# Moving the start addresses of a streaming encoder's matmul operands relative to the weights, by padding

## The chip, the cores and the metric

The kernel runs on one core of one Trainium2 chip. The metric is the time of one execution on the device, in microseconds. Where a profile is quoted, it is of one execution of the same program, with its own time.

## The reference, cut to what matters

The reference is one layer of a streaming encoder for 256 prompt tokens and 32 sample tokens, 288 together, at a model width of 2048, in float32. Nearly all of its arithmetic is products of the 288 tokens with weight matrices:

```python
h = rmsnorm(x, norm_in)
(a_q, a_k, a_v, i_q, i_k, i_w, a_z, b_z, b_xbc, b_dt, m_q, m_z, gates) = split_cols(h @ w_in)
...
mkv = rmsnorm(mem_prompt, norm_mem) @ w_mem_kv          # 256 memory tokens
...
merged = g_a * (ya @ w_pa) + g_b * (yb @ w_pb) + g_m * (ym @ w_pm)
return x + merged @ w_o, ...
y = rmsnorm(..., norm_final)
```

Between them stand three branches: sparse attention over keys picked by an indexer (`ya`), a Mamba-2 scan (`yb`) and cross-attention into the memory tokens (`ym`). They are small beside the products and run on the other engines and in short matmuls between those of the products.

## The kernel before, in words

Activations lie transposed: 128 channels on the partitions, and for each block k of 128 channels a row of 288 tokens along the partition, 1,152 bytes. A tile of 16 blocks is [128, 16, 288]. Weights come from memory as strips: 128 output columns by 1,024 input channels, 512 KB at a time, into `wr`.

Precision is kept by splitting. Each float32 number is written as a high part (`fp32r`, a rounded form) and a low part, the rest. `split_hi` (L119) and `split_lo` (L122) do this for activations. `convert` (L175 to L201) does it for weights: it takes the next job, issues the load of `wr` (L185), lets ScalarE write the high weights `wh` (L199) and VectorE the low ones `wl` (L200). So every product is three: high activations by high weights, low activations by high weights, high activations by low weights.

`strip` (L132 to L150) makes the jobs of a product. In a job of 1,024 channels there are 24 matmuls into one PSUM tile `ps`: for each of eight blocks i a pair, the high rows and then the low rows against `wh`, and after these the eight high rows against `wl` in the reverse order. The stationary operand (the one loaded by LDWEIGHTS) is the 128x128 block of weights, the moving operand is the row of 288 tokens; every matmul has its own weight load. The blocks go in the order `EVEN_ODD = (0, 2, 4, 6, 1, 3, 5, 7)`, and the weights of odd blocks lie in a second half of their tile:

```python
wh = wpool.tile([P, 1088], F32R, tag="wh", name="wh")                        # L186
wh = bass.AP(tensor=wh.tensor, offset=wh.offset, ap=[wh.ap[0], [544, 2], [P, 4], [1, P]])   # L191
```

The second half begins 544 elements, 2,176 bytes, behind the first. A row of 288 tokens is 1,152 bytes. Modulo 256 both of them put the odd ones 128 bytes behind the even ones.

`run` (L258) works the list of jobs off: for each, it converts the weights of a later one, issues the 24 matmuls, and calls `step`, which lets the side work (attention, scan, norms: Python generators) issue its next piece. The order of jobs is: memory keys (`w_mk`, strips over the memory tokens, rows of 256 tokens, 1,024 bytes), memory values (`mv_block`, L152: here blocks of `memh` and `meml` are the loaded operand, and 512 columns of weights move), then `w_in` in 133 strips of two jobs, with `w_pm`, `w_pa`, `w_pb` and `w_o` (16 strips each) where their inputs are ready.

The moving tiles are these. `xh` and `xl`, high and low rows of the normed input, come from the pool `const` (L76, L77), which is laid out in the order of the calls, one tile behind the other; `mgh` and `mgl`, the merged branches, take the same places at the end (L1063, L1064). The others are slots A to H of the pool `big`, given out by `slot` (L64): A and B hold `memraw` and `memh` at first and the pair `yb` for `w_pb` later; C holds `meml` and later other things; E and F hold the memory keys and values, then the pair `ym` for `w_pm`, then the pair `ya` for `w_pa`; D, G and H hold float32 tiles that no high or low row is in. Between `const` and `big` lies `wpool` with three buffers each of `wr` (4,096 bytes), `wh` and `wl` (4,352 bytes, 17 times 256); pools lie in the order of L41 to L46. In this layout `xh`, `xl`, every `wh` and `wl`, and each slot start at 128 modulo 256.

Of the kernel before, what the change touches and what calls it, by code (L numbers as in the profile page):

```python
# [7 lines left out]
F32 = mybir.dt.float32  # L8
F32R = mybir.dt.float32r
# [4 lines left out]
P = 128  # L14
TP = 256
TS = 32
T = TP + TS
# [16 lines left out]
def step_kernel(ctx, tc, ins, outs):  # L34
    nc = tc.nc
    V, S, G, PE = nc.vector, nc.scalar, nc.gpsimd, nc.tensor
    PS = bass.MemoryType.PSUM

    const = ctx.enter_context(tc.tile_pool(name="const", bufs=1))
    wpool = ctx.enter_context(tc.tile_pool(name="wpool", bufs=3))  # L40
    big = ctx.enter_context(tc.tile_pool(name="big", bufs=1))  # L41
# [19 lines left out]
    def st(n=8):  # L61
        return stp.tile([P, n], F32, tag="st", name="st")

    def slot(tag, shape, dt=F32):  # L64
        return big.tile(shape, dt, tag=tag, name=tag)

    def mm(out, lhsT, rhs, start=True, stop=True):
        PE.matmul(out, lhsT, rhs, start=start, stop=stop)  # L68
# [1 line left out]

    N = Names()
    N.memraw = slot("A", [P, 16, 256])
    N.memh = slot("B", [P, 16, 256], F32R)
    N.meml = slot("C", [P, 16, 256], F32R)
    N.x = slot("D", [P, 16, T])
    xh = const.tile([P, 16, T], F32R, name="xh", tag="xh")  # L76
    xl = const.tile([P, 16, T], F32R, name="xl", tag="xl")  # L77
    X = (xh, xl)

    S.preload_act_table_set("natural_log_exp_and_others")  # L80
    nc.sync.dma_start(N.memraw[:, 0:4], ins["memT"][:, 0:4])
    cols = const.tile([P, 288], F32, name="cols")
    S.dma_start(cols[:, 0:272], ins["cols"])
    g_mem, g_in, g_ssm, g_fin, d_col = (cols[:, 16 * i:16 * i + 16] for i in range(5))
    cw = cols[:, 80:176].rearrange("p (c i) -> p c i", c=24)
# [439 lines left out]
    dt = const.tile([P, 96], F32, name="dt")  # L525
# [534 lines left out]
    proj(N_G, ev_gb)  # L1060

    def begin_pb():
        N.mg = (const.tile([P, 16, T], F32R, name="mgh", tag="xh"),  # L1063
                const.tile([P, 16, T], F32R, name="mgl", tag="xl"))  # L1064

    def ev_pb(j):
# [9 lines left out]
        return f  # L1076

    hook(begin_pb)
    for j in range(16):
        strip([ins["w_pb"][j, h] for h in range(2)], "yb", ev_pb(j))  # L1080
# [137 lines left out]
```

## Time and profile before

| what | value |
|---|---|
| median of three runs | 1363.24 us (1363.21 to 1363.25) |
| the profiled execution's own time | 1363.02 us |
| its span, first to last instruction | 1361.3 us |
| granted TensorE clock, mean | 0.996 |
| TensorE matmul, busy | 98% of the span, 10,082 instructions |
| weight loads, busy | 96% |
| VectorE, ScalarE, GpSimd busy | 56%, 45%, 17% |
| read from HBM | 223.06 MB, 169 GB/s over the span with what is written |

On the profile page PE is the matmul row of TensorE and PEld its weight loads, which overlap the matmuls. DVE is VectorE, ACT is ScalarE, POOL is GpSimd. Matmuls are pipelined, so the busy time of one (some 295 ns) is not what it costs: the cost is the distance from its start to the start of the next, which is read from the timeline, or from a stretch of the chain of waits divided by its count.

### The profile page before, as it was taken

The page shows a single profiled execution, that of the slowest core. Times are in us where ns is not written, and L with a number is a line of the kernel's source. Part 1 is how long each engine was busy: PE and PEld are TensorE (multiplying, and loading weights), DVE is VectorE, ACT ScalarE, POOL GpSimd, SP SyncE. Part 2 cuts the span into 40 slices and gives each one's busy share as a digit, 9 for nine tenths or more (in the row PEclk, how much of TensorE's full clock was granted, in tenths as well). Part 3 has the DMA queues.
Part 4 walks back from the last instruction along what each step waited for, and adds up shares of the span by engine and source line. Part 5 has one row for each costly group of instructions (what it writes and reads, how often), then busy time and mean ns, then how long its engine had stood idle before and what let it go on. Part 6 is the DMA issues. An engine that isn't in the chain of part 4 may idle for free.

```text
span 1361.3 us, 24483 instructions
## 1 busy us (share of the span) xinstructions
PE 1335.1 (98%) x10082; PEld 1305.1 (96%) x10082; DVE 768.6 (56%) x1166; ACT 606.6 (45%) x859; POOL 237.1 (17%) x319
## 2 busy tenths in 40 slices
PE   6999999999999999999999999999999999999995
PEld 6989999899999999999999999999999999999995
DVE  7674345585567767646556546753444434555444
ACT  5554353434556543725435336553333433334331
POOL 4501000000000001132231233500043000001433
PEclk9999999999999999999999999999999999999998
DMA  8667434344434444664545454444446444455442
GB/s 290 210 221 250 156 121 142 128 155 158 168 140 151 148 162 163 221 192 157 183 146 183 158 178 146 167 172 168 157 171 233 165 174 161 156 173 170 169 170 85
DMA packets 63007, 232.05 MB, mean 170 GB/s; under 512 B 7264, under 2 KB 7808, under 8 KB 61744
## 3 DMA queue, kind: packets, MB, share of 16 engines
q1 hardware_dynamic: 57888, 209.72, 44.9%
q0 software_dynamic: 4144, 19.30, 4.3%
q8 instruction: 79, 1.29, 0.4%
q10 hardware_dynamic: 864, 1.47, 0.3%
q14 instruction: 32, 0.26, 0.1%
HBM read 223.06 MB, written 7.33 MB: 169 GB/s over the span
## 4 chain that ended last, share of the span: by engine, by line
PE 98%; DVE 1%; DMA 1%; ACT 0%; issue 0%; DVEq 0%; SPq 0%; ACTq 0%
PE ps L68 91%; PE sd L68 5%; DMA A<-in_memT 1%; DVE A L1111 0%; PE sd L879 0%; PE sd L745 0%; DVE C L281 0%; PE sd L863 0%; PE sd L453 0%; DVEq L1196 0%; ACT F L327 0%; PE sd L689 0%; ACT B L280 0%; ACT t L104 0%; ACT t L608 0%
## 5 line engine op out<-in xcount | busy, mean ns | idle before, releaser
L200 DVE TENSOR_TENSOR wl<-wr,wh 128x1024 fp32r<-128x1024 f32 x394 | 492.4, 1255 | 386.6 <-ACT wh L199 385.5
L68 PE MATMUL ps<-xh,wh 128*128 128x288 f32 x2128 | 579.0, 298 | 0.0
L68 PE MATMUL ps<-xl,wh 128*128 128x288 f32 x2128 | 570.5, 295 | 0.0
L199 ACT ACTIVATE wh<-wr 128x1024 fp32r<-128x1024 f32 x394 | 412.0, 1054 | 233.9 <-PE ps L68 182.7
L68 PEld LDWEIGHTS ps<-xh,wh 128*128 128x128 f32 x2128 | 399.5, 188 | 7.5 <-issue 3.2
L68 PEld LDWEIGHTS ps<-xl,wh 128*128 128x128 f32 x2128 | 399.8, 188 | 1.3 <-issue 0.7
L68 PE MATMUL ps<-xh,wl 128*128 128x288 f32 x2128 | 325.4, 295 | 0.0
L68 PEld LDWEIGHTS ps<-xh,wl 128*128 128x128 f32 x2128 | 297.3, 188 | 0.0
L68 PE MATMUL ps<-B,wh 128*128 128x288 f32 (+1 forms) x384 | 102.6, 296 | 8.8 <-ACT wh L199 8.4
L68 PEld LDWEIGHTS ps<-B,wh 128*128 128x128 f32 x384 | 74.0, 193 | 9.2 <-ACT wh L199 8.4
L68 PE MATMUL ps<-E,wh 128*128 128x288 f32 x256 | 69.5, 298 | 0.0
L68 PE MATMUL ps<-mgl,wh 128*128 128x288 f32 x256 | 68.8, 295 | 0.0
L68 PE MATMUL ps<-A,wh 128*128 128x288 f32 x256 | 68.8, 295 | 0.0
L68 PE MATMUL ps<-mgh,wh 128*128 128x288 f32 x256 | 68.8, 295 | 0.0
L68 PE MATMUL ps<-F,wh 128*128 128x288 f32 x256 | 68.7, 295 | 0.0
L808 POOL COPY cso<-t 128x3 f32<-128x3 f32 x24 | 5.2, 216 | 255.1 <-ACT t L806 255.1
L68 PEld LDWEIGHTS ps<-E,wh 128*128 128x128 f32 x256 | 48.0, 188 | 1.1 <-issue 0.8
L68 PEld LDWEIGHTS ps<-F,wh 128*128 128x128 f32 x256 | 48.1, 188 | 0.2 <-issue 0.2
L68 PEld LDWEIGHTS ps<-A,wh 128*128 128x128 f32 x256 | 48.1, 188 | 0.0
L68 PEld LDWEIGHTS ps<-mgh,wh 128*128 128x128 f32 x256 | 48.1, 188 | 0.0
L68 PEld LDWEIGHTS ps<-mgl,wh 128*128 128x128 f32 x256 | 48.1, 188 | 0.0
L68 PE MATMUL ps<-A,wl 128*128 128x288 f32 x256 | 39.2, 295 | 0.0
(293 smaller groups left out, 1337.2 us busy)
## 6 DMA issues: line engine op xcount, KB each, us to landing
wr<-in_w_in SPq DMA_DIRECT2D x266, 512.0 KB, 3.3
wr<-in_w_pb SPq DMA_DIRECT2D x32, 512.0 KB, 3.5
wr<-in_w_o SPq DMA_DIRECT2D x32, 512.0 KB, 3.3
wr<-in_w_mk SPq DMA_DIRECT2D x16, 512.0 KB, 4.2
wr<-in_w_mv SPq DMA_DIRECT2D x16, 512.0 KB, 4.3
wr<-in_w_pm SPq DMA_DIRECT2D x16, 512.0 KB, 3.3
wr<-in_w_pa SPq DMA_DIRECT2D x16, 512.0 KB, 3.3
B<-scr POOLq DMA_DIRECT2D x4, 1152.0 KB, 9.3
```

The lines of the kernel that those rows point to most:

```text
L68: PE.matmul(out, lhsT, rhs, start=start, stop=stop)
L199: S.activation(wh, raw, AF.Copy)
L200: V.tensor_tensor(wl, raw, wh.bitcast(F32), OP.subtract)
L808: G.tensor_copy(cso[:, c, 0:3], u[:, 256:259])
```

## The change

No instruction is added, removed or moved in the order. Addresses change, by padding:

- `slot` asks for a tile that is up to 224 bytes longer and uses it from an offset: 160 bytes for A, 32 for B, 224 for E, 32 for F, none for the others.
- `xh` (and `mgh` later) becomes 4,616 elements long, of which the first 4,608 are used: what follows it in `const` lies 32 bytes later.
- `cols` becomes 304 elements long instead of 288: what follows it lies 64 bytes later still.

```diff
+    SHIFT = {"A": 160, "B": 32, "E": 224, "F": 32}
+
     def slot(tag, shape, dt=F32):
-        return big.tile(shape, dt, tag=tag, name=tag)
+
+        o = SHIFT.get(tag, 0) // 4
+        n = {"E": 2304, "F": 2304, "G": 2304, "H": 2304}.get(tag, 4608)
+        t = big.tile([P, n + o], dt, tag=tag, name=tag)
+        m = 1
+        for d in shape[1:]:
+            m *= d
+        t = t[:, o:o + m]
+        return t if len(shape) == 2 else t.rearrange("p (a b) -> p a b", a=shape[1])
...
-    xh = const.tile([P, 16, T], F32R, name="xh", tag="xh")
+    def high():
+        return const.tile([P, 4616], F32R, name="xh", tag="xh")[:, 0:4608].rearrange("p (k t) -> p k t", k=16)
+
+    xh = high()
     xl = const.tile([P, 16, T], F32R, name="xl", tag="xl")
...
-    cols = const.tile([P, 288], F32, name="cols")
+    cols = const.tile([P, 304], F32, name="cols")
...
-        N.mg = (const.tile([P, 16, T], F32R, name="mgh", tag="xh"),
+        N.mg = (high(),
                 const.tile([P, 16, T], F32R, name="mgl", tag="xl"))
```

## The prediction, made before the changed kernel ran

> **What bounds the kernel now.** I read the page first: the busy times, the clock, the shares of the chain that ended last.
>
> ```profile
> PE 1335.1 (98%) x10082; PEld 1305.1 (96%) x10082; DVE 768.6 (56%) x1166; ACT 606.6 (45%) x859; POOL 237.1 (17%) x319
> PEclk9999999999999999999999999999999999999998
> PE 98%; DVE 1%; DMA 1%; ACT 0%; issue 0%; DVEq 0%; SPq 0%; ACTq 0%
> ```
>
> TensorE carries 98% of the chain, at full clock in all slices but the last. Then the waits of TensorE: if another engine held it up, it would stand here. These two are the longest, both in the first microseconds.
>
> ```profile
> PE ps L68 <- ACT wh L199: 8.4, 1, 8.4
> PE ps L68 <- DVE C L281: 2.1, 2, 1.6
> ```
>
> So the time is the number of matmuls times the distance from one start to the next. Third, the groups by line, for the counts of the matmuls with 288 columns.
>
> ```profile
> L68 PE MATMUL ps<-xh,wh 128*128 128x288 f32 x2128 | 579.0, 298 | 0.0
> L68 PE MATMUL ps<-xl,wh 128*128 128x288 f32 x2128 | 570.5, 295 | 0.0
> L68 PE MATMUL ps<-xh,wl 128*128 128x288 f32 x2128 | 325.4, 295 | 0.0
> L68 PE MATMUL ps<-E,wh 128*128 128x288 f32 x256 | 69.5, 298 | 0.0
> L68 PE MATMUL ps<-F,wh 128*128 128x288 f32 x256 | 68.7, 295 | 0.0
> L68 PE MATMUL ps<-E,wl 128*128 128x288 f32 x256 | 39.1, 295 | 0.0
> ```
>
> The pairs A and B (`yb`) and `mgh` and `mgl` have 32 jobs each as E and F have, so 768 matmuls too. Together 3 x 2,128 + 3 x 768 = 8,688. Fourth, the chain in order of time, for the distance: a stretch divided by its count.
>
> ```profile
> 44.70 11.52 PE ps L68 x96
> 180.51 3.45 PE sd L68 x16
> 411.36 9.46 PE ps L68 x72
> 425.62 9.53 PE ps L68 x72
> 893.91 451.56 PE ps L68 x3408
> 1351.33 6.00 DVE A L1111 x9
> ```
>
> The long stretch is 3,408 matmuls without a break, 132.5 ns each. 8,688 of these are 1,151 us of the span of 1,361. That is the only term large enough to matter, and the change touches exactly its addresses.
>
> **How much of the 132.5 ns could be given back.** The row at 44.70 is from the memory keys, rows of 256 columns: 120.0 ns each. The memory values move 512 columns; their timeline is here, six distances from 70.44 to 71.80.
>
> ```profile
> 70.44 0.39 PE L68 MATMUL ps<-wh,B 128*128 128x512 f32 x1
> ...
> 71.80 0.39 PE L68 MATMUL ps<-wh,B 128*128 128x512 f32 x1
> 180.34 3.61 PE L68 MATMUL sd<-t,F 128*128 128x256 f32 x16
> ```
>
> That is 1.36 / 6 = 226.7 ns for 512 columns. From 256 to 512 columns: 106.7 ns more, 0.417 ns a column. 256 columns at that rate are 106.7 ns, so 13.3 ns of the 120.0 do not depend on the length; at 288 columns it is 132.5 - 120.0 = 12.5 ns. The last row, with the row at 180.51 of the chain, is the control. It is plain float32 in the side work, 16 matmuls of 256 columns with a weight load each, 3.45 / 16 = 215.6 ns. If a column takes twice the time there (213.3 ns), only 2.3 ns are left over. So a weight load before each matmul costs little by itself. The other 10.2 ns of the 12.5 appear only where the moving row is read at the fast rate. My reading is that the load of the next weights and the moving row, read from the same memory at the same time, get into each other's way. Two more pieces speak for that reading.
>
> ```profile
> 1136.47 0.30 PE L68 MATMUL ps<-xh,wh 128*128 128x288 f32 x1
> 1136.61 0.30 PE L68 MATMUL ps<-xl,wh 128*128 128x288 f32 x1
> 1136.74 0.30 PE L68 MATMUL ps<-xh,wh 128*128 128x288 f32 x1
> 1136.88 0.29 PE L68 MATMUL ps<-xl,wh 128*128 128x288 f32 x1
> 1136.88 0.19 PEld L68 LDWEIGHTS ps<-xh,wh 128*128 128x128 f32 x1
> 604.66 0.29 PE L68 MATMUL ps<-xl,wh 128*128 128x288 f32 x1
> 604.78 0.29 PE L68 MATMUL ps<-xh,wh 128*128 128x288 f32 x1
> ```
>
> The load starts with the matmul that runs before its own (both at 1136.88). And equal matmuls are not equally far apart: three distances from 1136.47 take 0.41 us, 137 ns each; the one at 604.66 takes 0.12 us. With nothing else in its way TensorE would have no reason to vary between equal matmuls. Also the two chain rows of 72, three jobs each of the same stage: 131.4 against 132.4 ns, at the same addresses.
>
> The Trainium skill (TensorE: Matmul & The Clock Gate, Back-to-back issue gap) gives N / 2.4 + 2.5 ns for an isolated matmul, 122.5 ns for 288 columns. By it the excess would be 10.0 ns and the ceiling of this change 87 us; the trace agrees with its rate (0.417 ns a column), and shows no 288-column stretch near its sum.
>
> **What the change does to the addresses.** No instruction is added or removed, so the counts above stand. Worked out from the sizes of the tiles, modulo 256: in before, all start at 128, so a moving row lies 0 past its weights, and stays at 0 for all blocks, because odd rows and odd weights are both 128 further. (At the change from even to odd blocks the load is 128 off, twice in a job of 24.) After: `xh` stays at 128, `xl` is 32 later (160), all behind `cols` is 96 later, so `wh` and `wl` are at 224. `xh` is 128 - 224 = 160 past the weights, `xl` 192. A: 224 + 160 = 128, again 160; B: its tile begins at 128, + 32 = 160, so 192. C and D begin at 160. E: 160 + 224 = 128, so 160 past; F 192. So it does what it says for all 8,688. Not for the memory part: `memh` lies in B and `meml` in C, both 192 past the even blocks' weights, and with rows of 1,024 bytes 64 past the odd ones'. These 384 matmuls, and the 192 of the memory values, I take at nothing either way; at the 2.5 ns below they would be 1.4 us.
>
> **What that is worth.** Two group rows give the speed of a load.
>
> ```profile
> L68 PEld LDWEIGHTS ps<-A,wh 128*128 128x128 f32 x256 | 48.1, 188 | 0.0
> L68 PEld LDWEIGHTS sd<-G,A 128*64 128x64 f32 x128 | 7.5, 137 | 0.0
> ```
>
> 64 columns more take 51 ns more, 0.80 ns a column: about half the speed of the moving row. So while a load walks its 512 bytes in some 102 ns, the moving row walks 1,024, and gains 512 on it: two rounds of 256. If memory repeats every 256 bytes, the two come together every time that the lead grows through a multiple of 256. Starting at 0 that is at the start, in the middle and at the end of the load. Starting 160 or 192 ahead, it is twice, both well inside (96 or 64 bytes of lead later, and 256 after that). If the three meetings of before cost the same, each is 10.2 / 3 = 3.4 ns and one is gone; if those at the two ends count half, nothing changes in the sum, two full ones remain. I take a value between, nearer to the first, 2.5 ns, because a matmul that is held up at its start has no row read ahead to live on; it is also where the change would bring every matmul to 130 ns, a little under the best stretch of before (131.4). That is an estimate, and the weakest step: 8,688 x 2.5 = 21.7 us. The bounds on each side: if all of the 10.2 ns goes, 88.6 us; at the other end, 137 ns for each, as the three distances above, + 4.5 ns, 39 us slower.
>
> Nothing else should take that gain back. The weights are made in time with ease:
>
> ```profile
> 1133.30:1235.10 101.80, 101.80 (x771) 101.80 (x770) 55.18 (x75) 37.76 (x48) 0.00 (x0) 1.00 0.50 165
> 300.00:420.00 120.00, 120.00 (x911) 119.74 (x910) 73.39 (x124) 64.07 (x105) 3.72 (x24) 1.00 0.46 155
> ```
>
> The first is the stage of `w_pb`: VectorE is busy 55.18 us of 101.80, ScalarE 37.76, DMA at half. The second holds the convolution: VectorE 61%, ScalarE 53%. A stage that is 2% or even 8% shorter leaves both in its cover, and with it any cost of the new start addresses to them and to the loads, which I therefore count at nothing. If that cover were gone, 1% on VectorE's 768.6 us would be 7.7 us. The chain's tail behind the last matmul (from 1,345.5 to the end, some 16 us) is untouched.
>
> Sum: the profiled execution took 1363.02 us, its span and 1.7 us around it; the median of the runs is 1363.24, so both scales are the same within 0.2 us. 1363.0 - 21.7 = 1341.3 us.
>
> **Rivals.** *No effect.* The two reads are independent, and the 12.5 ns are a fixed price of swapping weights at the fast rate; or meetings cost the same wherever they fall. In both cases 0, 1363 us. For it: 12.5 and 13.3 ns are nearly the same at three lengths, and the count of rounds, two, doesn't depend on where they begin. Against it: the varying distances, and the control at half rate. The Trainium skill (SBUF — State Buffer, Who interferes with whom) speaks for this rival: the matmul's moving operand and the weight load have a read port each, and TensorE waits on no one; the varying distances don't look like it, but no row shows the reads themselves.
>
> *Slower, by locking in.* In before the distances vary because the meetings fall at other moments each time, and the good ones (0.12 us) pull the mean down. Where rows are 1,024 bytes, so that all falls alike, the trace shows 13.3 ns, not 12.5. If the new offsets lock every matmul into that, it is + 0.8 ns: 7 us, 1370 us. If the stream gets under way late, so that a lead of 64 to 96 bytes puts a third meeting inside a load, it is + 3.4 ns: 29.5 us, 1393 us. It decides from 132.8 ns a matmul. For it: 0 may be the good place, since the trace has next to no other offset to compare.
>
> *Much more.* The offsets leave one short meeting: two thirds of 10.2 ns go, 6.8 x 8,688 = 59 us, 1304 us. Against it: no stretch of before comes near 125.7 ns.
>
> **How the numbers follow.** 0.2% is 2.7 us, about what a measurement of this kernel can tell from no change. One meeting less or part of it, 1320 to 1360 us: 0.50. Much more: 0.12. No effect within 2.7 us: 0.13. Slower: 0.25, most of it the small lock-in. So faster 0.62, same 0.13, slower 0.25. The forecast's own range is 1320 to 1360. The range that holds 8 in 10 reaches past the lock-in on one side, to 1374, and to the case of much more on the other, 1300; beyond the upper end I leave about 0.11, beyond the lower 0.08.
>
> **What would show it.** Right: the same 10,082 matmuls, and in the chain a long stretch of 3,408 with some 130 ns each, 443 us instead of 451.56; PEclk and the counts unchanged; waits of TensorE still a few microseconds. Each of the stages should be shorter by the same share, about 2%, and the plain float32 row still at 215.6 ns. Wrong: 132.5 ns again (no effect), or 133.3 and more (locked in). If the stretches are shorter but the span isn't, a wait on `wh` or `wl` will stand in TensorE's waits, and the cover failed. If distances become equal over a job, the offsets took away the variation; if they still vary between 126 and 137, the phase between the two reads is set by something other than the addresses.

## The result, and the profile after

The changed kernel takes 1353.05 us (median of four runs, 1352.42 to 1353.31) against 1363.22 us for the kernel before on the same chip, a ratio of 0.9925 (95% interval 0.9908 to 0.9943). That is 10.2 us faster: the direction of the forecast, and just under half of its 21.7 us.

The page of the changed kernel, the same three lines as before (busy times, clock, chain by engine):

```profile
PE 1323.4 (98%) x10082; PEld 1292.9 (96%) x10082; DVE 769.6 (57%) x1166; ACT 606.9 (45%) x859; POOL 240.2 (18%) x319
PEclk9999999999999999999999999999999999999998
PE 96%; DVE 1%; POOL 1%; issue 1%; DMA 1%; ACT 0%; DVEq 0%; SPq 0%; POOLq 0%; ACTq 0%
```

TensorE is the bound as before, with the same counts and the same clock. Its busy time is 11.7 us shorter, the span 9.8 us (1351.5 against 1361.3). The chain in order of time and the waits of TensorE, two views of the same kernel:

```profile
888.82 446.88 PE ps L78 x3408
1341.56 6.00 DVE A L1124 x9
```

```profile
PE ps L78 <- ACT wh L212: 10.1, 2, 9.2
PE ps L78 <- DVE C L294: 2.6, 2, 1.6
```

The long stretch of 3,408 matmuls took 451.56 us and takes 446.88: 132.50 ns each are now 131.13, 1.37 ns less. The tail of nine is the same 6.00 us.

Half of the gain (4.68 us) comes from this stretch, 142 jobs at 33 ns a job. The other 220 jobs of the products, between which side work runs, give the other 5.1 us, 23 ns a job. There the kernel before was not always at its worst. A job's 24 matmuls have 23 distances from start to start; "inner" below means all but the first, 22 of them. Reading the starts of the matmuls job by job, in before they add up to 2,919 to 2,921 ns in 272 of the 362 jobs and to 2,892 to 2,894 in 49, at the same addresses. Such a job comes first behind a piece of side work, and a few more of them can follow. After the change 311 jobs have 2,884 or 2,885.

Within a job the distances are not equal, and they are not random either. In the long stretch before the change 141 of 142 jobs repeat the same 23 distances to within 1 ns, from 128 to 137 ns. After it, 140 of 142 do, with another sequence, from 127 to 137. So the prediction's sign "if they still vary" came true, but not what it was to mean: here the addresses set the sequence, and not the moment at which a job starts.

The memory part is not in this sum at all, though its matmuls changed most. A timeline there, first of the kernel before, then of the changed one (256 columns; 14 distances each):

```profile
50.35 0.28 PE L68 MATMUL ps<-B,wh 128*128 128x256 f32 x1
...
52.02 0.28 PE L68 MATMUL ps<-B,wh 128*128 128x256 f32 x1
48.75 0.28 PE L78 MATMUL ps<-B,wh 128*128 128x256 f32 x1
...
50.33 0.28 PE L78 MATMUL ps<-B,wh 128*128 128x256 f32 x1
```

They are 1.58 / 14 = 113 ns apart where they were 1.67 / 14 = 119. (Whole jobs have 118.9 before; the prediction's 120.0 comes from a stretch whose first distance, behind side work, is longer.) But the weights are not ready sooner. The stretch from 13.6 to 56.2 us, first in the kernel before, then in the changed one (busy times of TensorE, its loads, VectorE, ScalarE, GpSimd):

```profile
13.60:56.20 42.60, 42.60 (x336) 42.55 (x337) 33.30 (x39) 23.87 (x41) 23.59 (x24) 1.00 0.66 236
```

```profile
13.60:56.20 42.60, 41.05 (x336) 40.58 (x337) 32.99 (x40) 23.72 (x41) 27.00 (x24) 1.00 0.65 234
```

TensorE stands idle for 1.55 us that it was busy before, with the same number of matmuls. What it waits for is `wh`, behind the squares of the input norm on ScalarE, which wait for GpSimd's sums to free their buffers. The chain of the changed kernel goes through these sums. Its last pieces before the wait ends:

```profile
46.99 2.75 issue
...
50.34 1.26 POOL ev L355
...
51.97 1.05 ACT wh L212
...
53.06 3.08 PE ps L78 x24
```

The longest of these pieces, 2.75 us of "issue", is not a sum. GpSimd has to start the write of the memory keys to memory, and stands there until VectorE has scaled them in `E`:

```profile
49.75 0.56 POOL L331 DMA_DIRECT2D out_mem_k<-E  x1 [2.77 <-DVE E L329]
```

In the kernel before it stands there as long (2.77 us), and ScalarE makes the same weights at 51.78 us; now it is 51.97. So the 1.6 us that the memory keys gained turned into a wait. It is so in other kernels too. Of the twelve whole kernels, these two and the ten below, six have memory keys at 113 ns, and their products begin at 106.1 to 106.8 us; in the six with 118 to 119 ns they begin at 106.1 to 107.2. The longest wait on `wh`, 9.2 us against 8.4 before, is the one for the first weights, and need not come from the change: it is 9.2 us too in a run whose memory part has the addresses of before (the first map below). The memory values (512 columns) became 2 ns slower each, some 229 for 226.7.

### The profile page after: what moved, and what is told of

The parts are those of the page before. It is cut to its first block, busy times and chain, and to the rows that moved or that the text cites. A ratio compares the mean times of both kernels' runs of the same rounds, so it can differ in the third digit from the quotient of the medians.

```text
span 1351.5 us, 24486 instructions
## 1 busy us (share of the span) xinstructions
PE 1323.4 (98%) x10082; PEld 1292.9 (96%) x10082; DVE 769.6 (57%) x1166; ACT 606.9 (45%) x859; POOL 240.2 (18%) x319
## 4 chain that ended last, share of the span: by engine, by line
PE 96%; DVE 1%; POOL 1%; issue 1%; DMA 1%; ACT 0%; DVEq 0%; SPq 0%; POOLq 0%; ACTq 0%
PE ps L78 90%; PE sd L78 5%; POOL ev L355 1%; DMA A<-in_memT 1%; DVE A L1124 0%; PE sd L892 0%; DVE C L294 0%; PE sd L758 0%; PE sd L876 0%; PE sd L466 0%; ACT wh L212 0%; DVEq L1209 0%; ACT B L293 0%; ACT ev L353 0%; ACT F L340 0%
## 5 line engine op out<-in xcount | busy, mean ns | idle before, releaser
L78 PE MATMUL ps<-xh,wh 128*128 128x288 f32 x2384 | 644.3, 298 | 0.0
L78 PEld LDWEIGHTS ps<-xh,wh 128*128 128x128 f32 x2384 | 448.4, 188 | 7.5 <-issue 3.5
L78 PE MATMUL ps<-xh,wl 128*128 128x288 f32 x2384 | 360.9, 293 | 0.0
L78 PEld LDWEIGHTS ps<-xh,wl 128*128 128x128 f32 x2384 | 327.7, 188 | 0.0
L78 PE MATMUL ps<-E,wl 128*128 128x288 f32 x256 | 38.7, 293 | 0.0
```

## The experiments

Ten whole kernels and five maps, one run each but for the last two kernels, which have four. The kernel before, run beside them, took 1362.5 to 1365.3 us. For whole kernels the same stretch of the chain, 3,408 matmuls, is the best measure: side work doesn't touch it. "Lead" is how far a moving row's start lies past its weights' start, modulo 256, high rows first: (0, 0) is the kernel before, (160, 192) the changed one. A kernel with a pair of leads is the changed kernel with other pads, as in the short diffs.

### Everything 96 bytes later

```diff
+    const.tile([P, 24], F32, name="lead")
     xh = high()
```
(and no other pads: SHIFT all 0, `cols` 288, `xh` 4,608)

> Every tile starts 96 bytes later than in the kernel before, so the weights stand at 224 modulo 256 as in the changed kernel, but high and low rows lie 0 past them again. If only the lead of the moving row over the weights counts: 132.5 ns a matmul, 1363 us. If the place of the weights itself counts (absolute addresses): 131.2 ns, about 1353 us.

```profile
893.77 451.56 PE ps L78 x3408
```

To the last digit the stretch of the kernel before; 1362.89 us, beside 1364.22 for the kernel before on that chip. The distances within a job come back too, to within 1 ns. Starting at 224 modulo 256 instead of 128 does nothing. What the change brought comes from the leads.

### The two halves of the change, and both rows alike

```diff
-    SHIFT = {"A": 160, "B": 32, "E": 224, "F": 32}
+    SHIFT = {"A": 160, "B": 96, "E": 160, "F": 96}     # (160, 0)
+    SHIFT = {"A": 0, "B": 192, "E": 64, "F": 192}      # (0, 192)
+    SHIFT = {"A": 192, "B": 0, "E": 0, "F": 0}         # (192, 192)
```
(with the pads of `xh` and `cols` to match)

> High rows 160 past the weights, low rows 0. High rows move in two of three matmuls. If each matmul's cost depends on its own lead alone (meetings), two thirds of the 11.2 us that the products gained: 1356 us. If the pair of leads counts, because one row follows another in the stream, the two parts don't add up: anything from slower than 1363 to faster than 1353 us.

> Low rows 192 past the weights, high rows 0; the memory rows 192 as in the changed kernel. If each matmul's own lead counts: one third of 11.2 us, about 1359 us. If the pair counts, no sum: e2's and this one's changes together differ clearly from 10 us.

> High and low rows both 192 past the weights. By the meetings any lead well clear of 0 is as good as another: 131.2 ns a matmul, 1352 to 1354 us. If the pair counts (a high row's end against a low row's start), it differs from the changed kernel by more than 2 us in either direction.

One line of each chain, in this order:

```profile
895.23 450.62 PE ps L78 x3408
```

```profile
891.02 447.80 PE ps L78 x3408
```

```profile
898.40 453.47 PE ps L78 x3408
```

High rows alone give 0.28 ns a matmul (1363.42 us), low rows alone 1.10 ns (1356.37 us), both at 192 cost 0.56 ns (1369.42 us, slower than before). High rows move in two of three matmuls, and yet the low ones bring nearly all. These two halves do add up to the whole (0.94 + 3.76 = 4.70 us of the stretch against 4.68); the third kernel doesn't fit. A lead of 192, which was good for the low rows, is bad for both. No one cost per lead, the same for every matmul, can do both, and the meetings of the prediction fall: 192 is as clear of 0 as 160 is.

### A second theory: the seam between one row and the next

The memory keys at leads of 192 and 64 went to 113 ns. Their rows are 1,024 bytes, so each begins, modulo 256, where the one before it ended. With 288 columns a pair of leads that differ by 128 makes high and low rows do so.

```diff
-                for i in EVEN_ODD[::-1]:
+                for i in reversed(range(8)):       # third kernel only
```

> High rows 64, low rows 192 past the weights. A row of 288 columns ends 128 past its start modulo 256, so here a high row ends where the low row begins and a low row where the next high one begins, as in the memory keys, whose 1,024-byte rows do so anyway and took 113.3 ns at leads 192 and 64. If the seam between two moving rows counts (new theory), the 16 matmuls on the high weights come down to 113.3 + 13.3 = 126.7 ns, the 8 on the low weights, where a high row follows a high row, stay near 132: 362 jobs save 16 x 5.8 = 93 ns each against before, 1363 - 34 = 1330 us. If only each row's own lead counts (the meetings), no better than the changed kernel: 1352 to 1357 us.

> The mirror: high rows 192, low rows 64 past the weights. The seams fit here too, so by the seam theory the same as with 64 and 192, about 1330 us. If the own lead counts and 192 is bad for a high row (both at 192 was 1369 us), slower than 1363 us.

> High 64, low 192, and the eight matmuls on the low weights go through the blocks 7, 6, 5 ... 0 instead of 7, 5, 3, 1, 6, 4, 2, 0, so that each high row begins where the one before it ended modulo 256. By the seam theory all but one or two of the 24 then take 126.7 ns: 362 x 24 x 5.8 less than before, 1363 - 50 = 1313 us. If the seam doesn't count: no more than 2 us from the kernel with 64 and 192 alone.

> High rows 0, low rows 128 past the weights: the seams fit, but the rows lead by 0 or 128, as the memory keys did in the kernel before, which took 119 ns for 256 columns, so 119 + 13.3 = 132 ns here. If the seam alone is enough: about 1330 us. If seam and lead both count: 1360 to 1366 us.

The stretch in these four, in this order:

```profile
893.07 449.68 PE ps L78 x3408
```

```profile
894.70 450.63 PE ps L78 x3408
```

```profile
893.33 449.69 PE ps L78 x3408
```

```profile
894.61 450.16 PE ps L78 x3408
```

1360.32, 1362.88, 1360.57 and 1362.33 us: all within 0.6 ns a matmul of the kernel before, none near 126.7. The order of the blocks on the low weights changes 0.01 us. The seam theory fell too.

### A map of leads

One kernel can try many pairs: `strip` is given a list and reads the rows of `w_in` at an offset inside `xh` and `xl`. Weights and rows stay where they are in the kernel before.

```diff
+                    hi[k], lo[k] = fh[:, r + a:r + a + w], fl[:, r + b:r + b + w]   # a, b by the job; r = 288 k
```

> A map, in the place of 64 kernels: in the product with w_in the moving rows are read at an offset, 0 to 224 bytes in steps of 32 for the high and for the low rows, each of the 64 pairs in four jobs; the numbers of the products are therefore those of shifted rows, not the reference's, and the last block's row is read in another's place. If each row's own lead counts (meetings), a job's time is a sum of a term for the high and a term for the low lead, and all pairs clear of 0 are alike. If the phase in which a row and a load meet is handed on from one matmul to the next, the map is irregular, with 3149 ns a job at (160, 192), 3180 at (0, 0), 3196 at (192, 192) as in the runs so far, and no sum of two terms fits it.

The mean of the 22 inner distances of a job (from the starts of the matmuls in the trace, the second lowest of four jobs), ns:

```
high \ low    0     32     64     96    128    160    192    224
   0       132.8  132.0  132.1  131.5  132.2  133.0  131.4  132.9
  32       133.0  133.7  132.4  133.5  133.0  133.3  132.7  133.3
  64       131.9  131.9  131.5  132.4  132.0  132.2  132.0  132.3
  96       133.6  133.1  132.5  131.5  133.0  132.5  132.6  132.7
 128       131.9  132.4  132.2  133.6  133.0  132.8  132.7  133.5
 160       132.4  133.3  132.5  132.0  132.5  133.6  131.1  132.2
 192       131.8  132.1  132.1  132.6  132.1  132.1  133.2  132.3
 224       133.0  133.0  132.2  133.3  133.4  131.0  132.0  133.6
```

The map can be trusted: the whole kernels, measured in the same way, have 132.7 at (0, 0), 132.2 at (160, 0), 131.4 at (0, 192), 131.1 at (160, 192), 133.2 at (192, 192), 132.0 at (64, 192), 132.1 at (192, 64) and 132.3 at (0, 128). All agree within 0.2. A term for the high lead plus a term for the low lead leaves 64% of the variance unexplained. And it shows how small the prize was: the best of 64 pairs is 131.0, and the change's pair, at 131.1, is as good as that.

### Lengths, and smaller loads

> The same map with 320 columns in each matmul of w_in instead of 288 (32 more of the next row; results are not the reference's): 1,280 bytes, five times 256. If what holds the 288-column matmuls above the memory keys' best (6.7 ns over the columns) is that 1,152 bytes are not a multiple of 256, so that row and load never settle, here good pairs settle: 133.3 + 6.7 = 140.0 ns each, 3360 ns a job, and bad ones at 133.3 + 13.3 = 146.7, 3520. If length plays no such part, the pattern of the 288 map moves up by 13.3 ns a matmul, 3149 + 320 = 3469 ns for (160, 192).

With 320 columns all 64 pairs lie between 145.5 and 148.1 ns, 12.2 to 14.8 above the columns (at the prediction's 0.417 ns each). None comes to 140.0, so a length that is a multiple of 256 bytes doesn't settle it either.

The next map goes through lengths, and through loads of fewer columns.

```diff
+                        mm(box["p"][0:lc, 0:w], wh[:, i % 2, i // 2, 0:lc], at(fl, k0 + i, b, w), False, False)
```

> A second map over the jobs of w_in, four jobs each: the number of columns from 192 to 512 at leads (0, 0) and (160, 192); weight loads of 32 and 64 columns instead of 128 at 288 moving columns; the lead of the high rows over the low weights varied by itself, 0 to 224 bytes; leads in steps of 16 around (160, 192). Rows are shifted, cut or lengthened and part of the outputs is not computed, so the numbers of the products are not the reference's. If what stands above the columns (12.5 ns) is the load and the row getting into each other's way, it shrinks with the load: 127 to 128 ns with 64 columns loaded, 124 to 126 with 32. If it is a fixed price of changing weights, 132.5 ns with any load. If the leads decide by themselves, (160, 192) is better than (0, 0) at every length; if it is the phase, which a length changes as much as a lead, the difference changes its sign from length to length and the excess swings between 6 and 16 ns. By the phase, the lead over the low weights matters as much as the others, up to 1.5 ns a matmul, and the best of these slots is 1 to 2% under the changed kernel's job; by the leads alone at most the 8 matmuls on the low weights change.

Loads of 32 columns, their row in the group of loads, and 14 distances of such a job in the timeline:

```profile
L68 PEld LDWEIGHTS ps<-xl,wh 128*32 128x32 f32 x23 | 2.5, 108 | 0.5
```

```profile
599.13 0.29 PE L68 MATMUL ps<-xl,wh 128*32 128x288 f32 x1
...
600.97 0.29 PE L68 MATMUL ps<-xl,wh 128*32 128x288 f32 x1
109.52 0.27 PE L68 MATMUL ps<-xl,wh 128*128 128x192 f32 x1
...
110.63 0.27 PE L68 MATMUL ps<-xl,wh 128*128 128x192 f32 x1
```

The load takes 108 ns instead of 188, a quarter of the columns, and the matmuls are still 1.84 / 14 = 131.4 ns apart (over all inner distances 131.2; with 64 columns 129.9, with 128 columns 132.6). So at 288 columns the 12.5 ns are not paid per column loaded; at (160, 192) smaller loads are even slower, 132.3 ns with 64 columns and 131.6 with 32 against 130.8 with 128. The last two rows are at 192 moving columns: ten distances in 1.11 us, 111 ns. Below 240 columns a shorter row is no faster. By length, the mean of 20 inner distances, ns:

```
columns    192    240    256    272    288    304    320    384    448    512
(0,0)    111.6  112.0  119.3  126.1  132.6  138.6  146.6  173.7  206.4  227.7
(160,192) 111.7  111.7  118.8  124.6  130.8  138.8  145.7  175.1  203.4  232.5
```

The pair (160, 192), 1.8 ns better than (0, 0) at 288 columns, is 1.4 worse at 384 and 4.8 worse at 512. What a lead is worth depends on the length of the rows. The excess over 0.417 ns a column swings from 11 to 20 ns. The lead of the high rows over the low weights, varied alone, gave no slot under 130.7, nor did steps of 16 bytes around (160, 192).

### Steps of four bytes

> A third map over the jobs of w_in (rows shifted, cut or lengthened, part of the outputs not computed; not the reference's numbers): columns from 260 to 304 in steps of 4 at leads (0, 0) and (160, 192); both leads from 4 to 60 bytes in steps of 4; 256 columns at several leads; loads of 16 to 112 columns. In the map before this one the matmuls seemed to begin on a grid of 6.67 ns, the time of 16 columns (64 bytes of the moving row): with 64 columns loaded they were 127 and 133 ns apart in turn. If rows are read in steps of 64 bytes, the time of 276 to 288 columns is the same (132.6 ns at (0, 0)) and jumps at 292. If it is linear, 1.67 ns for every 4 columns, 127.6 at 276. If the place within 64 bytes counts, leads of 4 to 60 are worse than 0 by part of a step; if they are alike, no. For 256 columns at (192, 192) or (64, 64): 113.3 ns as in the memory keys if the leads alone made that, about 119 if it took the memory keys' change of lead between even and odd blocks.

The 6.67 ns grid fell: 276, 280, 284, 288, 292 and 296 columns at (0, 0) take 125.9, 128.5, 133.1, 132.6, 133.5 and 136.2 ns, neither a stair nor a line. 256 columns at (192, 192) take 116.7 and at (64, 192) 117.5, not 113. This map also has smaller loads at 256 columns, and there they do count. Fourteen distances at (0, 0) with 64 columns loaded:

```profile
949.79 0.28 PE L68 MATMUL ps<-xl,wh 128*64 128x256 f32 x1
...
951.38 0.28 PE L68 MATMUL ps<-xl,wh 128*64 128x256 f32 x1
```

That is 1.59 / 14 = 114 ns, where 128 columns loaded take 119.3. The means are 114.2 with 64, 114.6 with 32 and 115.0 with 16. So at 256 columns about 5 of the 12.6 ns above the columns go away with half the load, and no more with less; at 288 columns 2.7 do with half and 1.4 with a quarter. But the steps of four bytes showed an order where steps of 32 had shown none. With equal leads x, ns by x modulo 16:

```
0 mod 16:    0 132.6   16 131.9   32 133.5   48 131.8   mean 132.4
4 mod 16:    4 135.5   20 134.0   36 134.7   52 135.9   mean 135.0
8 mod 16:    8 133.7   24 134.9   40 133.1   56 134.0   mean 133.9
12 mod 16:  12 131.7   28 130.3   44 130.0   60 133.1   mean 131.3
```

### Rows at 12 modulo 16

> A map of 128 pairs of leads, two jobs of w_in each (rows shifted, not the reference's numbers): high and low rows at 12 + 32 k, and at 28 + 32 k. In the map of steps, leads that are 12 modulo 16 were the best of their group (130.0 ns at 44, 130.3 at 28), 4 modulo 16 the worst (134 to 136). If the place within 16 bytes is what counts, all 128 pairs lie at 129 to 132 ns, mean under 131.5, against 132.5 for the 64 pairs at multiples of 32. If that was chance, as the irregular map would have it, their mean is 132.5 again with the same spread of some 0.7.

The first line of the page of the map of pairs at multiples of 32, and of this one:

```profile
span 1362.8 us, 24483 instructions
```

```profile
span 1351.4 us, 24483 instructions
```

The kernel with these 128 pairs is 11.4 us shorter than the one with the 64 at multiples of 32. Job by job the mean of the inner distances is 131.1 ns (130.0 to 133.5) against 132.6 (130.8 to 134.0). So the place within 16 bytes is no chance: it is worth 1.5 ns on average. The rest stays irregular.

> A whole kernel with high and low rows both 44 past the weights (the weights begin 20 bytes into their tile, and the pads are 192 and 64 bytes). If the map carries over to a kernel, 130.0 ns a matmul instead of 132.6 at (0, 0): 8,688 x 2.6 = 22.6 us less than before, 1340 to 1343 us, and 7 to 10 us less than the changed kernel. If the weights' odd start costs their writers or the small offset doesn't hold across stages: 1350 us or more.

```diff
-            wh, wl = (bass.AP(tensor=w.tensor, offset=w.offset, ap=[w.ap[0], [544, 2], [P, 4], [1, P]])
+            wh, wl = (bass.AP(tensor=w.tensor, offset=w.offset + 5, ap=[w.ap[0], [544, 2], [P, 4], [1, P]])
```
(with the other pads to match)

```profile
912.66 462.91 PE ps L78 x3408
```

135.8 ns a matmul, 1393.13 us, ratio 1.0216 (1.0199 to 1.0233): the slowest of the whole kernels, at leads that had 130.0 ns in the map. TensorE's waits are as in before, so no engine came late, and a weight load takes the same 188 ns. What differs is which operand is off 16 bytes. In the map the rows begin at 12 modulo 16 and the weights at 0; here the rows are at 0 and the weights at 4. The lead isn't everything: moving both by 96 bytes changes nothing, moving both back by 44, from the place in the map, does.

> High rows 28 and low rows 60 past the weights, reached by shifting the rows inside their tiles (28 bytes) and not the weights, which stay on a multiple of 32. The map of fine pairs had 2861 ns for the 22 inner distances of such a job, 130.0 ns each, against 2884 in the changed kernel. If the map carries over when it is the rows that are shifted, 131.1 - 130.0 = 1.1 ns on 8,688 matmuls, 9 us under the changed kernel's 1353: 1343 to 1346 us. If the kernel with 44 and 44 was slow because leads off 16 don't carry over to a kernel at all, 1380 us or more; if rows off a 16-byte place slow down the engines that write them and they come late, waits on wh, wl or the rows appear and the time stays above 1353.

```diff
+        return const.tile([P, 4616], F32R, name=name, tag=tag)[:, 7:4615].rearrange("p (k t) -> p k t", k=16)   # xh, xl, mgh, mgl
-    SHIFT = {"A": 160, "B": 32, "E": 224, "F": 32}
+    SHIFT = {"A": 28, "B": 28, "E": 220, "F": 28}
```
(with the other pads to match)

```profile
883.62 443.06 PE ps L78 x3408
```

```profile
PE ps L78 <- ACT wh L212: 9.1, 2, 8.5
```

```profile
L213 DVE TENSOR_TENSOR wl<-wr,wh 128x1024 fp32r<-128x1024 f32 x394 | 492.9, 1256 | 377.1 <-ACT wh L212 370.4 <-PE ps L78 5.7
```

130.0 ns a matmul, as the map said; 1343.78 us, ratio 0.9861 (0.9844 to 0.9877), 9 us under the changed kernel. No wait is new, and VectorE takes 1,256 ns for the low weights, where the kernel before has this row with 1,255:

```profile
L200 DVE TENSOR_TENSOR wl<-wr,wh 128x1024 fp32r<-128x1024 f32 x394 | 492.4, 1255 | 386.6 <-ACT wh L199 385.5
```

This version beats both kernels.

## Why the prediction was wrong, point by point

**The bound** was right: TensorE's distances from start to start are the time, all counts stayed, and 1.37 ns off each matmul of the long stretch came through to the span. **The addresses** were right, with the exception for the memory part. That no engine would come late was right for the products, and wrong for the memory keys, which I took at nothing: they gained 1.6 us and lost it to a wait for `wh`. That nothing was left of them in the sum is luck.

**The step that failed is the worth of a lead**: "I take a value between, nearer to the first, 2.5 ns" a matmul. It measured 1.37 ns in the long stretch and 9.8 us / 8,688 = 1.1 ns overall. It is not only the size. The reason behind it, meetings of a load and a row once per 256 bytes of lead gained, is refuted by four findings: high rows alone should have given two thirds and gave a fifth of the stretch's gain (0.94 of 4.68 us); both at 192 should have been as good and was slower than before; a load of a quarter of the columns should have removed most of the excess at 288 columns, and the matmuls stayed at 131 ns; and the excess changes with the length, which two rounds per load don't. Nor does any run show the reason given for a value nearer to 3.4 ns, that a matmul held up at its start has no row read ahead.

So the direction was luck as well. By the same reason every pair with both leads clear of 0 would gain. In the map 18 of these 49 are slower than (0, 0), and (160, 192) happens to be the second best of all 64.

**The control misled.** From plain float32 (215.6 ns, 2.3 over the columns) I concluded that swapping weights is nearly free and that 10.2 ns were there to be won. At 288 columns the runs found no pair anywhere near that: of 64 pairs the best was 131.0 ns, and with rows off 16 bytes 130.0. (At 256 columns more could be won, 5.6 ns in the memory keys.) A control at half the rate doesn't show what is free at the full one.

**The rivals.** "No effect" is refuted: only addresses changed, and the stretch ran at anything from 130.0 to 135.8 ns a matmul. The rule that I set beside it, from the Trainium skill (SBUF — State Buffer, Who interferes with whom), that row and load have a port each and TensorE waits on no one, is not enough to tell the time here: (192, 192) is 6.6 us slower than (160, 192) in the long stretch alone, and only addresses differ. Whether the two reads meet anywhere, no run shows. The rival's other half, a fixed price of swapping weights, comes nearer than mine did: it says why at 288 columns a load of 32 costs about as much as one of 128, but not why addresses matter, nor why a smaller load helps at 256. A slower pair exists, not this one but (192, 192), 133.06 ns; whether by locking in is not shown. The prediction's ground for a lock-in falls: rows of 1,024 bytes took 118.9 ns, which at its 0.417 ns a column is 12.2 over the columns, not 13.3. "Much more" was nowhere.

**What stays open** is the mechanism. Shown is what the cost depends on: the pair of leads, not each lead; the length of the row; at 256 columns the size of the load; and the place of rows and weights within 16 bytes. That points to a state which one matmul hands on to the next, as do the two patterns (2,893 and 2,919 ns) at the same addresses, of which one outlasts the side work that it began behind. What that state is, no run here shows.

## What to carry to other kernels

When a kernel is bound by matmuls with a weight load each, their distance from start to start is worth reading to the nanosecond, and the start addresses of rows and weights are a knob of one or two per cent. It is a knob to be scanned, not reasoned about: one kernel that reads its rows at another offset in each job maps a hundred pairs in one run, and its values held to 0.2 ns in nine whole kernels. They failed in the tenth, whose weights did not begin on a multiple of 16 bytes. Scan in the steps of the element and at the kernel's own row length, since a pair that is good at 288 columns can be bad at 512. The one place off 16 bytes that was tried for the weights was the worst.

## What the runs showed of the hardware that was not expected

- Rows that begin at 12 modulo 16 bytes, with weights at 0, are the best group (131.1 ns over 128 pairs, 132.6 over 64 pairs at multiples of 32), those at 4 modulo 16 the worst (135.0, four equal pairs alone). The Trainium skill (SBUF — State Buffer, Specifications (TRN2)) gives lines of 16 bytes there. The runs agree that 16 is a period that counts; that an odd place is better than the line's start is not what one would take from it.
- Weights at 4 modulo 16 with rows at 0 made 135.8 ns a matmul, where the same leads with rows at 12 and weights at 0 had 130.0.
- With a load of 128 columns before each, matmuls were on average no closer than some 111.5 ns: 192, 208, 224 and 240 columns take the same within 0.6. Shorter rows with smaller loads were not tried.
- At 256 columns and leads (0, 0) a load of 64 columns brings 119.3 ns down to 114.2; at 288 columns it brings 132.6 down to 129.9, and one of 32 only to 131.2.
- In the long stretch, jobs repeat their 23 unequal distances to within 1 ns: 141 of 142 jobs before the change, 140 after it.
- The memory keys at leads of 192 and 64 run at 113 ns for 256 columns, near that floor, where the maps at (192, 192) and (64, 192) had 116.7 and 117.5; before, they took 119. Their worth was hidden behind a wait of 1.5 us.
